# The head of a two-layer decoder trunk: some first loads move from SyncE's queue to ScalarE's, SiLU moves behind a PSUM product, and the order of the first products and splits is written out

## The chip, the core and the metric

The kernel runs on one NeuronCore of one Trainium2 chip, in one launch. Its time is the device time in microseconds (us) of that launch; three runs of the kernel before gave 1242.72, 1240.34 and 1240.87 us, median 1240.87 us. The profile is one execution recorded by the hardware profiler, with its own time and with the span from its first instruction to its last. The engines are TensorE (PE in the profile, with its weight loads apart as PEld), VectorE (DVE), ScalarE (ACT), GpSimd (POOL) and SyncE (SP). SyncE computes nothing; in the kernel before every load of the stage that is looked at here is issued from its queue.

## The reference

The function is a hybrid decoder trunk of two layers on one sequence of 256 tokens with 2048 channels, in float32. The part that matters here is the adaLN step in front of layer 0: three vectors of 2048 are computed from the conditioning vector `c`, and two of them scale and shift `x` ahead of the first big product.

```python
def _adaln(c, w, b):
    mod = jax.nn.silu(c) @ w + b
    shift, scale, gate = jnp.split(mod, 3, axis=-1)
    return shift[:, None, :], scale[:, None, :], gate[:, None, :]

# layer 0
h = x * (1.0 + scale) + shift
proj = h @ in_w                      # (256, 2048) @ (2048, 10304)
z, xBC, dt = jnp.split(proj, ...)
...                                  # convolution, chunked state-space scan, gate, norm
y = y @ out_w
x = _layer_norm(DEEPNORM_ALPHA * x + (1.0 + gate) * y, ln_g[0], ln_b[0])
...                                  # shared K/V, layer 1 (dilated attention), output
```

## The kernel before

Weights are read from memory once, in float32. Each weight piece is 128 partitions by 1024 floats (512 KB). It is loaded into a tile `raw`, and split into two reduced-precision tiles: ScalarE writes the high part `whi` (L100), VectorE the remainder `wlo` (L102). The activations are split in the same way (`hhi` and `hlo`, the two halves of the tile `actT`). A product is then three TensorE passes: high by high, high by low, low by high (L151 to L153 where the channels end on partitions, L213 to L215 where the tokens do).

**Channels.** The 2048 channels of `x` are 16 tiles of 128, numbered `kt`. For every `kt` the function `h_step` runs twice: once for the scale column and once for the shift column of the modulation. A column is a 1 MB tile `araw` of adaLN weights; VectorE multiplies it by `cb_` (SiLU of `c`, spread over all 128 partitions) and adds up along the row (`ada_dot`, L296). For the very first column this is done in two halves of 1024 (L471 and L473), so that the first half needs only half of `cb_`. After the shift column the biases are added (L301), and ScalarE makes `htmp`, that is `x` scaled and shifted (L492), and its high part (L494); VectorE makes the low part (L496).

**Spreading c.** `c` comes as 16 rows of 128 with a 16 by 16 unit matrix beside it (`crow`, the tile called `prm` in the profile). Sixteen small TensorE products with a column of that unit matrix as stationary side (L443) copy each of the 16 rows to all 128 partitions, into four PSUM tiles `cps`; ScalarE copies them into `cb_` (L446). In the kernel before, SiLU is applied to `crow` first (L72), and the products take its result. Around them `warm` issues products of a tile of ones, whose results nobody reads (L435).

**First products.** The function `plain` (L541) multiplies the first channel tile (`kt` = 0) of the first three weight pieces in full float32, straight from `raw` and `htmp`, with no split. Only the second half of those pieces (`kt` = 1) is split, by `half` (L549 and L550). From then on the loop at L623 takes the pieces in the order of the list `order`; between pieces it calls `h_step`, so that channel tiles come into being while products with the earlier ones run. This goes on until about 171 us; then come the scan, the output product, shared K/V, layer 1 and the output.

**What sets the order.** Each engine executes its instructions in the order in which the program gives them to it; a planner may move an instruction of one engine ahead of another of the same engine unless `tc.issue_after(x)` pins it behind `x`. Each queue of loads is served by one engine: a load that must wait for a buffer or for an earlier load holds all loads behind it on the same engine. Each load signals one of eight counters (`DMAHW0` to `DMAHW7` in the listings); the next load that uses the same counter waits for the one before it. Buffers: `raw` has six, `araw` two in each of the pools `wp1` and `pe`, `whi` and `wlo` four each.

The fills at the head are in `fetch` (an `araw`), `fetch_x` (two channel tiles of `x`, 256 KB), `begin_piece` and `end_piece` (the two 256 KB halves of a piece) and `fetch_piece` (a whole piece). The biases are `adab_` (48 KB).

## Time and profile before

| | us |
|---|---|
| median of three runs | 1240.87 |
| lowest and highest run | 1240.34 and 1242.72 |
| time of the profiled execution | 1241.06 |
| its span, first to last instruction | 1239.3 |
| TensorE busy in the span | 1227.7 (99%) |
| VectorE busy | 1026.7 (83%) |
| ScalarE busy | 702.1 (57%) |
| first product with split operands (L151) | starts at 22.03 |

The profiled execution lies 0.19 us above the median of the runs. A timeline row gives start, length, engine, line, operation, output and inputs, how many instructions of the kind it merges, and in brackets the idle time of the engine just before it and what ended it. TensorE's busy time counts the products of ones as well, so 99% doesn't mean that 99% is needed work. A row of stretches gives, for each, the busy time of PE, PEld, DVE, ACT and POOL with the number of instructions, the granted TensorE clock (1.00 is full), the mean busy share of the 16 DMA engines, and what they moved in GB/s. An SPq row is SyncE issuing a load: its length is the time to issue, not the time to land.

### The profile page before, as it was taken

Reading aid. Unit: us, or ns where it says so; the run is one execution under the profiler, and the core shown is the slowest. Engines: PE = TensorE matmul, PEld = TensorE weight load, DVE = VectorE, ACT = ScalarE, POOL = GpSimd, SP = SyncE. Lnnn points to the kernel's source line nnn. Section 1 sums busy time; section 2 is a strip of 40 time slices with the busy share of each in tenths; the row PEclk is TensorE's granted clock in tenths of the full one; section 3 lists DMA queues with packets and bytes.
Section 4 is the critical chain, followed back from the end, with each engine's and each line's share of the span. In section 5 each row is a group of like instructions: output and inputs, shape, how many; then the busy total and the mean of one; then the engine's idle time right before and its main releaser. Section 6 shows DMA issues by size and latency. Waiting matters only on the chain.

```text
span 1239.3 us, 18924 instructions
## 1 busy us (share of the span) xinstructions
PE 1227.7 (99%) x7178; PEld 1056.4 (85%) x7178; DVE 1026.7 (83%) x1454; ACT 702.1 (57%) x1048; POOL 3.8 (0%) x8
## 2 busy tenths in 40 slices
PE   9999999999999999999999999999999999999998
PEld 9889998898888888887888788888888888888886
DVE  6999986999987989899768678889978867658776
ACT  4555477868597789764335544434445645445631
POOL 0000000000000000000000000000000000000001
PEclk9999999999999999999999999999999999999999
DMA  9999977687656456699998569989997784464753
GB/s 368 422 421 422 421 256 248 231 288 257 215 192 210 164 172 202 215 338 338 365 317 294 193 201 354 372 340 369 381 384 293 231 260 136 134 203 121 226 217 68
DMA packets 81051, 335.90 MB, mean 271 GB/s; under 512 B 9168, under 2 KB 9408, under 8 KB 68160
## 3 DMA queue, kind: packets, MB, share of 16 engines
q1 hardware_dynamic: 80384, 333.65, 74.9%
q0 software_dynamic: 576, 1.05, 0.6%
q8 instruction: 56, 0.92, 0.3%
q14 instruction: 35, 0.29, 0.1%
HBM read 331.43 MB, written 3.23 MB: 270 GB/s over the span
## 4 chain that ended last, share of the span: by engine, by line
PE 89%; DMA 4%; DVE 4%; ACT 2%; issue 1%; DVEq 0%; SPq 0%; ACTq 0%
PE acc L182 24%; PE acc L214 12%; PE acc L215 12%; PE acc L213 12%; PE acc L185 12%; PE acc L151 3%; PE acc L153 3%; PE acc L152 3%; DMA raw<-in_win 2%; DMA araw<-in_ada 1%; PE py L758 1%; DVE wlo L102 1%; DVE araw L296 1%; ACT whi L100 1%; PE acc L968 1%
## 5 line engine op out<-in xcount | busy, mean ns | idle before, releaser
L100 ACT ACTIVATE whi<-raw 128x1024 fp32r<-128x1024 f32 x389 | 408.1, 1058 | 359.3 <-PE acc L215 140.7
L102 DVE TENSOR_TENSOR wlo<-raw,whi 128x1024 fp32r<-128x1024 f32 x389 | 469.4, 1223 | 141.5 <-ACT whi L100 137.4
L182 PE MATMUL acc<-actT,whi 128*128 128x512 f32 x1280 | 405.3, 397 | 0.0
L185 PEld LDWEIGHTS acc<-actT,wlo 128*128 128x128 f32 x1280 | 239.4, 188 | 55.6 <-DVE wlo L102 0.4
L214 PE MATMUL acc<-wlo,actT 128*128 128x512 f32 x656 | 257.1, 392 | 1.4 <-DVE wlo L102 1.4
L213 PE MATMUL acc<-whi,actT 128*128 128x512 f32 x656 | 253.6, 394 | 0.0
L185 PE MATMUL acc<-actT,wlo 128*128 128x256 f32 x1280 | 252.8, 279 | 0.0
L296 DVE SCALAR_TENSOR_TENSOR araw<-araw,cb__72 128x2048 f32<-128x2048 f32 x95 | 217.0, 2287 | 3.7 <-DMA araw<-in_ada 3.4
L182 PEld LDWEIGHTS acc<-actT,whi 128*128 128x128 f32 x1280 | 195.9, 189 | 0.4
L215 PE MATMUL acc<-whi,actT 128*128 128x512 f32 x432 | 168.9, 391 | 0.0
L214 PEld LDWEIGHTS acc<-wlo,actT 128*128 128x128 f32 x656 | 123.2, 188 | 27.6 <-DVE wlo L102 2.6
L213 PEld LDWEIGHTS acc<-whi,actT 128*128 128x128 f32 x656 | 122.8, 188 | 24.2
L151 PE MATMUL acc<-actT,whi 128*128 128x256 f32 x372 | 105.0, 285 | 0.9 <-ACT whi L100 0.9
L152 PE MATMUL acc<-actT,whi 128*128 128x256 f32 x372 | 104.4, 283 | 0.0
L153 PE MATMUL acc<-actT,wlo 128*128 128x256 f32 x372 | 102.5, 284 | 1.6 <-DVE wlo L102 1.6
L215 PEld LDWEIGHTS acc<-whi,actT 128*128 128x128 f32 x432 | 81.1, 188 | 16.7
L215 PE MATMUL acc<-whi,ylo 128*128 128x512 f32 x224 | 87.6, 391 | 0.0
L151 PEld LDWEIGHTS acc<-actT,whi 128*128 128x128 f32 x372 | 71.3, 192 | 1.9 <-ACT whi L100 1.3
L153 PEld LDWEIGHTS acc<-actT,wlo 128*128 128x128 f32 x372 | 70.0, 192 | 2.2 <-DVE wlo L102 2.0
L152 PEld LDWEIGHTS acc<-actT,whi 128*128 128x128 f32 x372 | 71.3, 192 | 0.3
L215 PEld LDWEIGHTS acc<-whi,ylo 128*128 128x128 f32 x224 | 42.1, 188 | 8.6
L716 ACT ACTIVATE seg<-cbc,cumT 128x128 f32<-128x128 f32 x128 | 41.0, 389 | 4.9 <-DVE wlo L102 2.3
(289 smaller groups left out, 1159.6 us busy)
## 6 DMA issues: line engine op xcount, KB each, us to landing
araw<-in_ada SPq DMA_DIRECT2D x96, 1024.0 KB, 7.3
raw<-in_win SPq DMA_DIRECT2D x109, 512.0 KB, 6.1
raw<-in_wout SPq DMA_DIRECT2D x64, 512.0 KB, 5.8
raw<-in_wbin SPq DMA_DIRECT2D x64, 512.0 KB, 3.8
raw<-in_wxs SPq DMA_DIRECT2D x48, 512.0 KB, 4.5
raw<-in_wv SPq DMA_DIRECT2D x48, 512.0 KB, 6.2
raw<-in_wk SPq DMA_DIRECT2D x48, 512.0 KB, 7.4
cbc<-cumd SPq DMA_DIRECT2D x16, 512.0 KB, 4.7
```

The costliest lines, as they stand in the source:

```text
L100: copied.append(S.activation(hi, raw, AF.Copy))
L102: latest.append(V.tensor_tensor(lo, raw, hi.bitcast(F32), op=ALU.subtract))
L151: T.matmul(o, hi[:, k, c_], ahi[:, kt, :], start=first, stop=False, skip_group_check=True)
L152: T.matmul(o, hi[:, k, c_], alo[:, kt, :], start=False, stop=False, skip_group_check=True)
L153: T.matmul(o, lo[:, k, c_], ahi[:, kt, :], start=False, stop=kt == k1 - 1, skip_group_check=True)
L182: T.matmul(ps[n], hi[:, k, n * P:n * P + P], both(kt), start=kt == 0, stop=False, skip_group_check=True)
L185: T.matmul(ps[n][:, 0, :], lo[:, k, n * P:n * P + P], high(kt), start=False, stop=kt == KT - 1, skip_group_check=True)
L213: T.matmul(o, h_, hi[:, k, :], start=kt == k0, stop=False, skip_group_check=part)
L214: T.matmul(o, h_, lo[:, k, :], start=False, stop=False, skip_group_check=part)
L215: end = T.matmul(o, l_, hi[:, k, :], start=False, stop=kt == k1 - 1, skip_group_check=part)
L296: return V.scalar_tensor_tensor(raw, raw, 1.0, cb_, op0=ALU.mult, op1=ALU.mult, accum_out=mod[layer][:, ct, j:j + 1])
L716: S.activation(seg[:, hh, b, :], cbc[:, hh, b, :], AF.Relu, bias=cumT[:, b, h0 + hh:h0 + hh + 1], scale=-1.0)
```

## The change

All of it lies in the first 25 us of the program; behind that, the engines get the same instructions in the same order.

- **Queues.** The loads of `c`, of the first two channel tiles of `x`, of the biases and of the first halves of pieces 0 and 1 are issued from ScalarE. SyncE starts with four `araw` one behind the other, then the first half of piece 2, then the second halves.
- **SiLU.** `c` goes into the spreading products as it is; SiLU is applied when ScalarE takes the four PSUM tiles into `cb_`, in place of the copy.
- **Products.** `warm` and `plain` return their last product and take the one that they must come behind, so TensorE's order at the head is the written one: 6 products of ones, 16 spreading products, 13 of ones, the plain products of pieces 0 and 1, 4 of ones, those of piece 2, 4 of ones. In the source the counts were 6, 20, 5 and 5, free to be moved.
- **Splits.** `half` is divided into `high_half` (ScalarE) and `low_half` (VectorE). The high halves of pieces 0 and 1 come ahead of the second channel tile on ScalarE, and their low halves ahead of the low part of that channel tile on VectorE.
- One `fetch_piece` comes ahead of the plain products in the source; its place in SyncE's queue is the same.

```diff
-    nc.sync.dma_start(crow, c)
-    S.activation(crow[:, :P], crow[:, :P], AF.Silu)
+    nc.scalar.dma_start(crow, c)
...
-                def warm(n, at):
+                def warm(n, at, after=None):
                     for _ in range(n):
-                        T.matmul(at[:, 0, :P], ones, ones, start=True, stop=True)
+                        with tc.issue_after(after.ins) if after is not None else ExitStack():
+                            after = T.matmul(at[:, 0, :P], ones, ones, start=True, stop=True)
+                    return after
...
-                warm(6, at)
+                last = warm(6, at)
...
-                            T.matmul(cps[:, j * P:j * P + P],
-                                     crow[:, P + 4 * n + j:P + 4 * n + j + 1].to_broadcast([KT, P]),
-                                     crow[:, :P], start=True, stop=True)
-                        S.activation(cb_[:, 512 * n:512 * n + 512], cps, AF.Copy)
-                    warm(20, at)
+                            with tc.issue_after(last.ins):
+                                last = T.matmul(cps[:, j * P:j * P + P],
+                                                crow[:, P + 4 * n + j:P + 4 * n + j + 1].to_broadcast([KT, P]),
+                                                crow[:, :P], start=True, stop=True)
+                        S.activation(cb_[:, 512 * n:512 * n + 512], cps, AF.Silu)
+                    last = warm(13, at, last)
...
-                    nc.sync.dma_start(xts[kt // 2], xT[:, kt:kt + 2, :])
+                    (nc.sync if kt else nc.scalar).dma_start(xts[kt // 2], xT[:, kt:kt + 2, :])
...
-                    nc.sync.dma_start(pieces[i][:, :512], source[order[i][0]][order[i][1]][:, :512])
+                    (nc.scalar if i < 2 else nc.sync).dma_start(pieces[i][:, :512], source[order[i][0]][order[i][1]][:, :512])
...
-                fetch()
-                fetch()
                 fetch_x(0)
-                nc.sync.dma_start(adab_, par[:, :NB])
+                nc.scalar.dma_start(adab_, par[:, :NB])
                 begin_piece(0)
                 begin_piece(1)
-                fetch()
-                fetch()
+                for _ in range(4):
+                    fetch()
                 begin_piece(2)
...
-                plain(0)
-                plain(1)
+                last = plain(1, plain(0, last))
                 while late:
                     pin[0] = late.pop()().ins
-                fetch_piece()
-                warm(5, first[1][0])
-                plain(2)
-                warm(5, first[1][0])
+                last = warm(4, first[1][0], plain(2, warm(4, first[1][0], last)))
                 h_step()
-                h_step()
-                with tc.issue_after(h_step.bias.ins), tc.issue_after(h_step.high.ins):
-                    half(0)
-                while late:
+                high_half(0)
+                high_half(1)
+                with tc.issue_after(copied[-1].ins):
+                    h_step()
+                with tc.issue_after(h_step.bias.ins):
+                    low_half(0)
+                with tc.issue_after(latest[-1].ins):
+                    low_half(1)
+                with tc.issue_after(latest[-1].ins):
                     pin[0] = late.pop()().ins
-                with tc.issue_after(pin[0]):
-                    half(1)
-                    half(2)
+                with tc.issue_after(h_step.high.ins), tc.issue_after(pin[0]):
+                    high_half(2)
+                    low_half(2)
```

SyncE's queue at the head of the program, before (`prm` is `c`, `xt` the channel tiles of `x`, `adab` the biases, a 128x512 `raw` half a piece; in brackets the counters that a load waits for):

```order
L71 DMA prm<-in_c 16x144
L289 DMA araw<-in_ada 128x2048 x2
L460 DMA xt<-in_xT 128x512
L556 DMA adab<-in_par 128x96
L527 DMA raw<-in_win 128x512 x2
L289 DMA araw<-in_ada 128x2048
L289 DMA araw<-in_ada 128x2048 [waits DMAHW0_49]
L527 DMA raw<-in_win 128x512 [waits DMAHW1_49]
L530 DMA raw<-in_win 128x512 [waits DMAHW2_49]
```

And in the changed kernel:

```order
L288 DMA araw<-in_ada 128x2048 x3
L288 DMA araw<-in_ada 128x2048 [waits DMAHW0_49]
L529 DMA raw<-in_win 128x512 [waits DMAHW1_49]
L532 DMA raw<-in_win 128x512 [waits DMAHW2_49]
L532 DMA raw<-in_win 128x512 [waits DMAHW3_49]
L532 DMA raw<-in_win 128x512 [waits DMAHW4_49]
L93 DMA raw<-in_win 128x1024 [waits DMAHW5_49]
L288 DMA araw<-in_ada 128x2048 [waits DMAHW6_49,DVE_49]
```

Five loads have left SyncE's queue, and its first load is now the first `araw`. The counters 0, 2, 3, 4 and 5 for which it waits are those of the loads that ScalarE issues.

ScalarE's queue at the same place, before:

```order
L72 ACT_TABLE_LOAD
L72 ACTIVATE prm<-prm 16x128 [waits DMAHW0_49]
L446 ACTIVATE cb__72<-cps 128x512 [waits PE_49] x4
L492 ACTIVATE htmp<-xt,mod_84 128x256 [waits DMAHW3_49,DVE_49]
L494 ACTIVATE actT<-htmp 128x256 [waits Activation_49]
L492 ACTIVATE htmp<-xt,mod_84 128x256 [waits DVE_49]
L494 ACTIVATE actT<-htmp 128x256 [waits Activation_49]
L549 ACTIVATE whi<-raw 128x512 [waits DMAHW2_49]
```

And in the changed kernel:

```order
L71 DMA prm<-in_c 16x144
L462 DMA xt<-in_xT 128x512
L560 DMA adab<-in_par 128x96
L529 DMA raw<-in_win 128x512 x2
L448 ACT_TABLE_LOAD
L448 ACTIVATE cb__72<-cps 128x512 [waits PE_49] x4
L494 ACTIVATE htmp<-xt,mod_83 128x256 [waits DMAHW2_49,DVE_49]
L496 ACTIVATE actT<-htmp 128x256 [waits Activation_49]
L551 ACTIVATE whi<-raw 128x512 [waits DMAHW2_49]
L551 ACTIVATE whi<-raw 128x512 [waits DMAHW3_49]
L494 ACTIVATE htmp<-xt,mod_83 128x256 [waits DVE_49]
L496 ACTIVATE actT<-htmp 128x256 [waits Activation_49]
```

Five loads stand in front, the small SiLU is gone, and two high halves, which wait for the second halves of pieces 0 and 1 (SyncE's loads at L532), stand ahead of the second channel tile.

TensorE's queue, before (products of `ones` are the ones whose results nobody reads):

```order
L435 MATMUL acc<-ones 128x128 x10
L443 MATMUL cps<-prm 128x128 x16
L435 MATMUL acc<-ones 128x128 x23
L541 MATMUL acc<-htmp,raw 128x256 x8
L435 MATMUL acc<-ones 128x128 x3
L541 MATMUL acc<-htmp,raw 128x256 x4
L151 MATMUL acc<-actT,whi 128x256
L152 MATMUL acc<-actT,whi 128x256
```

And in the changed kernel:

```order
L435 MATMUL acc<-ones 128x128 x6
L445 MATMUL cps<-prm 128x128 x16
L435 MATMUL acc<-ones 128x128 x13
L544 MATMUL acc<-htmp,raw 128x256 x8
L435 MATMUL acc<-ones 128x128 x4
L544 MATMUL acc<-htmp,raw 128x256 x4
L435 MATMUL acc<-ones 128x128 x4
L150 MATMUL acc<-actT,whi 128x256
L151 MATMUL acc<-actT,whi 128x256
```

Ahead of the spreading products stand 6 products of ones instead of 10, behind them 13 instead of 23, and 4 and 4 instead of 3 and none around the plain products of piece 2. The profile shows each product of the head as two records.

More of the change, by code (lines that the diff above doesn't have):

```diff
@@ L532, in trunk, with plain @@
                 begin, done, ended, halves = {}, set(), [], {}
-                def plain(i):
+                def plain(i, after):
                     k = order[i][0]
@@ L540, in plain, with high_half, low_half @@
                     for n in range(4):
-                        T.matmul(pss[k][n // 2][:, n % 2, :], pieces[i][:, n * P:n * P + P], plain.t,
-                                 start=n % 2 == 0, stop=False, skip_group_check=True)
-                def half(i):
+                        with tc.issue_after(after.ins):
+                            after = T.matmul(pss[k][n // 2][:, n % 2, :], pieces[i][:, n * P:n * P + P], plain.t,
+                                             start=n % 2 == 0, stop=False, skip_group_check=True)
+                    return after
+                def high_half(i):
                     halves[i] = [wp.tile([P, 1024], F32R, name=n, bufs=4) for n in ("whi", "wlo")]
-                    hi, lo = (t[:, 512:1024] for t in halves[i])
-                    raw = pieces[i][:, 512:1024]
-                    copied.append(S.activation(hi, raw, AF.Copy))
-                    latest.append(V.tensor_tensor(lo, raw, hi.bitcast(F32), op=ALU.subtract))
+                    copied.append(S.activation(halves[i][0][:, 512:], pieces[i][:, 512:], AF.Copy))
+                def low_half(i):
+                    hi, lo = (t[:, 512:] for t in halves[i])
+                    latest.append(V.tensor_tensor(lo, pieces[i][:, 512:], hi.bitcast(F32), op=ALU.subtract))
                     halves[i] = [t.rearrange("p (k n) -> p k n", k=2) for t in halves[i]]
-                fetch()
-                fetch()
                 fetch_x(0)
-                nc.sync.dma_start(adab_, par[:, :NB])
+                nc.scalar.dma_start(adab_, par[:, :NB])
                 begin_piece(0)
                 begin_piece(1)
-                fetch()
-                fetch()
+                for _ in range(4):
+                    fetch()
                 begin_piece(2)
@@ L569, in trunk @@
                 fetch()
+                fetch_piece()
                 plain.t = h_step.t
[L571 to L572 removed]
+                last = plain(1, plain(0, last))
                 while late:
                     pin[0] = late.pop()().ins
[L575 to L578 removed]
+                last = warm(4, first[1][0], plain(2, warm(4, first[1][0], last)))
                 h_step()
[L580 to L583 removed]
+                high_half(0)
[7 more added lines that the diff above has]
+                with tc.issue_after(latest[-1].ins):
                     pin[0] = late.pop()().ins
[L585 to L587 removed]
+                with tc.issue_after(h_step.high.ins), tc.issue_after(pin[0]):
+                    high_half(2)
+                    low_half(2)
                 fetch_piece()
```

## The prediction

> **What bounds the kernel now.** I read the page first, then the stretches of the head, the chain that ended last, the waits, and the timelines of the first 25 us engine by engine.
>
> ```profile
> span 1239.3 us, 18924 instructions
> PE 1227.7 (99%) x7178; PEld 1056.4 (85%) x7178; DVE 1026.7 (83%) x1454; ACT 702.1 (57%) x1048; POOL 3.8 (0%) x8
> ```
>
> TensorE has 11.6 us without work in the whole span. A change at the head can give only what the head wastes, so the stretches come next.
>
> ```profile
> 0.00:2.00 2.00, 0.94 (x4) 0.95 (x5) 0.17 (x2) 1.27 (x1) 0.20 (x4) 1.00 0.02 5
> 2.00:4.00 2.00, 2.00 (x12) 2.00 (x11) 0.00 (x0) 0.33 (x2) 0.00 (x0) 1.00 0.85 238
> 7.00:12.00 5.00, 5.00 (x35) 4.78 (x34) 2.86 (x5) 2.35 (x4) 0.00 (x0) 0.74 0.99 334
> 12.00:58.00 46.00, 44.13 (x299) 40.77 (x298) 41.62 (x49) 24.21 (x37) 0.00 (x0) 0.99 1.02 421
> ...
> 22.03:58.68 36.65, 34.10 (x234) 31.35 (x233) 34.66 (x38) 22.24 (x34) 0.00 (x0) 1.00 1.02 421
> 58.68:182.00 123.32, 123.32 (x823) 113.98 (x824) 113.33 (x129) 70.72 (x91) 0.00 (x0) 1.00 0.97 387
> ```
>
> From 58.68 to 182 us TensorE is never idle: whatever moves its work at 58.68 us moves the end by as much. Between its first split product (22.03 us) and 58.68 us it is idle for 36.65 - 34.10 = 2.55 us, while the DMA engines are full (share 1.02, 421 GB/s). The chain says who ends that stage:
>
> ```profile
> 0.74 0.40 SPq L71
> 1.20 5.01 DMA araw<-in_ada
> 6.23 12.92 DMA raw<-in_win
> 34.00 13.02 DMA araw<-in_ada
> 47.04 2.31 DVE araw L296 x2
> 57.40 1.24 DVE wlo L102
> 58.68 0.39 PE acc L153
> ```
>
> The chain runs through landings: a column lands at 47.02 us, 13 us after it was issued, because everything issued before it is still going through full DMA engines. Behind it VectorE works nearly without a gap until the split that releases TensorE at 58.68 us. The waits from 20 to 58.8 us agree:
>
> ```profile
> ACT whi L100 <- DMA raw<-in_win: 12.9, 5, 4.2
> DVE wlo L102 <- ACT whi L100: 1.6, 3, 0.6
> ```
>
> So the time at 58.68 us is set by how early the DMA stream gets through its bytes; VectorE is close behind (34.66 of 36.65 us busy); TensorE has slack.
>
> **The change part by part: the DMA stream.** The bytes are the same, so it can only start sooner or run fuller in the first 12 us.
>
> - Start: the first `araw` is issued at 1.20 us, behind `c` at 0.74. With `c` on ScalarE it is issued at 0.74: 0.46 us gained.
> - Ramp: from 2 to 4 us the engines move 238 of 421 GB/s, a loss of 2 x (1 - 238/421) = 0.87 us.
> - Small rows: from 7 to 12 us they move 334, a loss of 5 x (1 - 334/421) = 1.03 us. This is when `x`, the biases and the half pieces come through.
>
> Two queues may fill these holes in part. The most is 0.46 + 0.87 + 1.03 = 2.36 us. The other end is a loss: no row shows two queues of loads side by side, and if their turns cost once more what the small rows cost, it is 1.03 - 0.46 = 0.57 us late. Between them I am guided by the DMA share: 0.85 and 0.99 while so little was moved. The engines were occupied, by rows that the change keeps. So I count a good third of 1.90 us, 0.7, as filled: 0.46 + 0.7 = 1.2 us gained (estimate).
>
> **TensorE, the spreading and SiLU.**
>
> ```profile
> 1.05 4.63 PE L435 MATMUL acc<-ones 128*128 128x128 f32 x20 [1.05 <-DVE magic L248]
> 5.62 4.08 PE L443 MATMUL cps<-prm 16*128 16x128 f32 x32
> 9.63 6.89 PE L435 MATMUL acc<-ones 128*128 128x128 f32 x46
> 16.36 3.62 PE L541 MATMUL acc<-htmp,raw 128*128 128x256 f32 x16
> 19.82 0.83 PE L435 MATMUL acc<-ones 128*128 128x128 f32 x6
> 20.49 1.89 PE L541 MATMUL acc<-htmp,raw 128*128 128x256 f32 x8
> 22.03 0.47 PE L151 MATMUL acc<-actT,whi 128*128 128x256 f32 x1
> ...
> 9.20:9.40 0.20, 0.20 (x4) 0.95 0.82 246
> 12.60:12.80 0.20, 0.20 (x3) 0.52 1.36 574
> ```
>
> The first 20 records take (5.62 - 1.05)/20 = 0.229 us each; the spreading ones 4.08/32 = 0.128. TensorE thus starts slow, although the clock column says 1.00 there, and the clock falls to half between 9.2 and 12.8 us. Six products of ones are 12 records: they end at 1.05 + 12 x 0.229 = 3.79 us, and spreading starts 1.83 us sooner. At the pace of before it ends at 7.87; at the slow pace it takes 32 x 0.229 = 7.33 us and ends at 11.12, 1.42 later than the 9.70 of before. I take the early value, since most of spreading ran fast in this trace, and keep both.
>
> ```profile
> 0.73 1.28 ACT L72 ACT_TABLE_LOAD   x1 [0.73 <-PEq L1306]
> 6.96 0.60 ACT L446 ACTIVATE cb__72<-cps 128x512 f32<-128x512 f32 x1 [4.36 <-PE cps L443]
> 14.23 0.60 ACT L492 ACTIVATE htmp<-xt,mod 128x256 f32<-128x256 f32 x1 [3.89 <-DVE mod L301]
> 20.39 0.60 ACT L492 ACTIVATE htmp<-xt,mod 128x256 f32<-128x256 f32 x1 [5.11 <-DVE mod L301]
> 21.35 1.66 ACT L549 ACTIVATE whi<-raw 128x512 fp32r<-128x512 f32 x3
> ...
> 10.37 1.23 DVE L473 SCALAR_TENSOR_TENSOR araw<-araw,cb__72 128x1024 f32<-128x1024 f32 x1 [0.65 <-ACT cb__72 L446]
> 21.48 0.42 DVE L496 TENSOR_TENSOR actT<-htmp,actT 128x256 fp32r<-128x256 f32 x1 [1.11 <-ACT actT L494]
> 21.99 1.90 DVE L550 TENSOR_TENSOR wlo<-raw,whi 128x512 fp32r<-128x512 f32 x3
> ...
> 2.12 0.43 SPq L460 DMA_DIRECT2D xt<-in_xT  x1
> 2.59 0.67 SPq L556 DMA_DIRECT2D adab<-in_par  x1
> 3.30 1.05 SPq L527 DMA_DIRECT2D raw<-in_win  x2
> ...
> L415 ACT ACTIVATE sz<-acc x4: 591/597/597, 334.0 to 515.0; 128x512 f32<-128x512 f32 x4
> ```
>
> - SiLU for copy: SiLU out of PSUM at 128x512 is 597 ns (L415), the copy 0.60: nothing. The small SiLU stood beside products of ones: nothing.
> - Five issues on ScalarE: 0.40 + 0.43 + 0.67 + 1.05 = 2.55 us at SyncE's prices, then the table load: 0.73 + 2.55 + 1.28 = 4.56 us. The first `cps` is there at 3.79 + (6.96 - 5.62) = 5.13 at the earliest: hidden, with 0.57 us to spare, beyond which it delays VectorE's first columns.
> - VectorE: its column halves wait for `cb_`, so they move by -1.83 to +1.42 us. Ahead of L496 it was idle for 1.11 us; two low halves (2 x 0.63 = 1.27) now fill that. By the third piece it stands at -2.94 to +0.31. Since it gets no piece before it lands, only the plus end reaches the total: between 0 and +0.3 in place of the gain.
> - Plain products: they started at 16.36, behind ones, though `htmp` was ready at 14.83. They can now start at about 13.0, or 16.3 at the slow pace. Behind that stand 3.62 + 1.89 and 16 records of ones at some 0.14 (0.83/6), 2.2 us: 7.7 in all, so the first split product comes at 20.7 to 24.0 instead of 22.03. Even +2.0 lies inside the 2.55 us of slack: nothing on the path.
> - High halves ahead of `htmp` on ScalarE: they wait for the second half of piece 1. The half ahead of it landed at 19.15 (6.23 + 12.92), so two more of 262 KB at 421 GB/s give 20.4 us, and 1.2 less in the changed kernel: 19.2, plus 0.55 (1.66/3) is 19.75, against `htmp` at 20.39. Behind it are queued `htmp` and its high part, for which L496 and the first split products wait. If the stream gained only 0.46 it would be 20.5, 0.1 late, inside TensorE's slack: nothing.
> - SyncE: waits for counters of ScalarE's loads. Its second half of piece 0 waits for `x`. With four `araw` ahead (4.2 MB, 10 us of DMA) this starves nothing unless `x` takes longer than those: nothing.
>
> Sum: -1.2 us. The profiled execution is 1241.06 us, its span 1239.3 with 1.76 around it, so 1239.9 on its scale; it is 0.19 above the median, so against 1240.87 the forecast is 1239.7 us.
>
> **The rivals.**
>
> *Two queues move no more than one.* The share of 0.99 at 334 GB/s speaks for it, the 0.85 of the ramp against. Only the 0.46 us of issue remains: 1240.4 us. [...]
>
> *The holes fill altogether.* 421 GB/s from 2 us on is 2.36 us, and with VectorE up to 2.9 us ahead some of its 1.6 us of waits for ScalarE goes too, say 0.4: 2.8 us, 1238.1. For it: VectorE's lead; against it: the shares again.
>
> *The slow clock stays through the spreading: slower.* The place is TensorE's 16 spreading products. For it: they feed 16 rows only, and the half clock came right after 3.4 us of mostly them; now 2.74 us of ones stand ahead in place of 4.57, which may not lift the clock at all. Then `cb_` is whole 1.42 us late and VectorE, +0.31 after filling its gap, sets the stage: 1241.2 us. From the point where the first split product comes after 22.03 + 2.55 = 24.6 us TensorE adds to it: each 3.4 us of half clock that reaches the plain products costs 1.7, so 24.0 + 1.7 = 25.7 gives 1.1 more, 1242.3; two such stretches 1244. Against it: ones and plain products are full arrays, and the clock rose over ones at 12.8.
> [...]
>
> **How the numbers follow.** Forecast (-0.5 to -2.0) 0.40; no more than one queue 0.18; holes filled 0.17; slow clock 0.23, of which 0.07 beyond its point; something I have not seen, slower, 0.02. What a measurement of this kernel can tell from no change is about 0.2%, 2.5 us: 1238.4 to 1243.4. Only the filled holes pass it downwards (0.17) and the far part of the slow clock and the unseen upwards (0.09); 0.74 lies within. The range 1238.0 to 1242.0 leaves out about half of the filled holes and the far part of the slow clock. The forecast's own range is 1238.9 to 1240.4.
>
> **What would show it.** Right: the first `araw` issued near 0.74; more than 334 GB/s from 7 to 12 us; `htmp` near 12.5 to 13.5; TensorE unbroken from about 57.5 instead of 58.68. Wrong: GB/s of the first 12 us as before (one queue's worth); spreading records at 0.229 us and `cb_` after 10.4 (slow clock); ScalarE waiting for the second halves beyond 20.5; the first split product after 24.6.

## The result: a little slower, and the profile after

The changed kernel takes 1243.51 us (median of 20 runs, 1241.69 to 1245.29) against 1241.01 for the kernel before (20 runs beside them, 1240.13 to 1243.84). The ratio is 1.0018 with a 95% interval of 1.0011 to 1.0025, which is 2.2 us (1.4 to 3.1). The forecast was 1239.7 us, with a range up to 1242.0. The profiled execution of the changed kernel took 1243.62 us.

The head of its page, and then its stretches (columns as in the prediction: the busy times of TensorE, of its weight loads, of VectorE, ScalarE and GpSimd, then the granted clock, the DMA share and GB/s):

```profile
span 1241.8 us, 18886 instructions
PE 1229.2 (99%) x7160; PEld 1057.8 (85%) x7160; DVE 1026.7 (83%) x1454; ACT 702.8 (57%) x1047; POOL 3.8 (0%) x8
```
```profile
2.00:4.00 2.00, 2.00 (x11) 1.76 (x9) 0.00 (x0) 0.58 (x1) 0.00 (x0) 1.00 0.81 304
4.00:7.00 3.00, 3.00 (x14) 3.00 (x15) 0.00 (x0) 1.30 (x2) 0.00 (x0) 1.00 0.99 399
7.00:12.00 5.00, 5.00 (x24) 4.78 (x23) 1.45 (x3) 1.79 (x3) 0.00 (x0) 1.00 1.00 380
12.00:17.00 5.00, 5.00 (x25) 4.99 (x24) 3.85 (x8) 1.02 (x2) 0.00 (x0) 1.00 1.01 402
17.00:18.00 1.00, 1.00 (x6) 0.89 (x5) 1.00 (x2) 0.42 (x1) 0.00 (x0) 1.00 0.68 258
18.00:19.00 1.00, 1.00 (x7) 0.87 (x6) 1.00 (x1) 0.85 (x2) 0.00 (x0) 1.00 0.97 158
19.00:20.00 1.00, 1.00 (x6) 0.90 (x5) 1.00 (x3) 0.00 (x0) 0.00 (x0) 1.00 0.90 328
```

The first 12 us went as hoped: 304 GB/s instead of 238 from 2 to 4 us and 380 instead of 334 from 7 to 12. Added up packet by packet, the changed kernel had moved 0.36 MB more than before by 14 us. Then something new shows: from 17 to 20 us the engines move 258, 158 and 328 GB/s. By 26 us the changed kernel is 0.31 MB behind, by 42 us 0.53 MB. The kernel before has no such hole: it moved 421 GB/s from 12 to 58 us.

What SyncE waited for in the first 30 us of the changed kernel, and its queue there:

```profile
SPq L532 <- DMA xt<-in_xT: 3.7, 1, 3.7
SPq L532 <- DMA raw<-in_win: 2.8, 1, 2.8
...
SPq L532 <- DMA adab<-in_par: 2.4, 1, 2.4
...
SPq L93 <- DMA raw<-in_win: 1.8, 2, 1.0
```
```profile
0.74 3.49 SPq L288 DMA_DIRECT2D araw<-in_ada  x4
5.70 0.33 SPq L529 DMA_DIRECT2D raw<-in_win  x1
9.78 6.22 SPq L532 DMA_DIRECT2D raw<-in_win  x3
17.05 0.33 SPq L93 DMA_DIRECT2D raw<-in_win  x1
17.50 0.36 SPq L288 DMA_DIRECT2D araw<-in_ada  x1
```

The first column is issued at 0.74 us, as forecast. But the three second halves (L532) wait for `x`, the biases and a half piece, all loads of ScalarE's queue: they go out between 9.78 and 16.00 us, only 0.26 MB each. The fourth piece waits once more, for the second half piece of ScalarE's queue, and goes out at 17.05; the fifth column follows at 17.50. In the meantime SyncE's earlier loads had been used up: that is the hole. Why those loads were so late is in the table of DMA issues of the first 20 us (KB each, median us from issue to landing) and in the queues' packets from 8 to 14 us:

```profile
raw<-in_win ACTq DMA_DIRECT2D x2, 256.0 KB, 13.8
xt<-in_xT ACTq DMA_DIRECT2D x1, 256.0 KB, 8.6
adab<-in_par ACTq DMA_DIRECT2D x1, 48.0 KB, 10.9
```
```profile
q1 hardware_dynamic: 286, 2.06, 83.0%
q10 hardware_dynamic: 288, 0.31, 16.5%
```

Both queues sent equally many packets, 286 and 288; but one of SyncE's holds 2.06 MB / 286 = 7.2 KB on average and one of ScalarE's 0.31 MB / 288 = 1.1 KB. ScalarE's loads therefore got 0.31 of 2.37 MB, and its last half piece landed at about 17 us.

The other rows that answer to the prediction's: TensorE's head, the copies into `cb_`, VectorE's wait for a column, and the release of TensorE, which was 58.68 us before.

```profile
1.05 2.93 PE L435 MATMUL acc<-ones 128*128 128x128 f32 x12 [1.05 <-DVE magic L247]
3.93 7.19 PE L445 MATMUL cps<-prm 16*128 16x128 f32 x32
11.05 5.91 PE L435 MATMUL acc<-ones 128*128 128x128 f32 x26
...
23.68 0.36 PE L150 MATMUL acc<-actT,whi 128*128 128x256 f32 x1
...
60.19 0.38 PE L152 MATMUL acc<-actT,wlo 128*128 128x256 f32 x1 [1.14 <-DVE wlo L101]
```
```profile
3.42 1.28 ACT L448 ACT_TABLE_LOAD   x1 [3.42 <-issue]
...
11.16 0.60 ACT L448 ACTIVATE cb__72<-cps 128x512 f32<-128x512 f32 x1 [1.11 <-PE cps L445]
...
17.58 1.27 ACT L551 ACTIVATE whi<-raw 128x512 fp32r<-128x512 f32 x2 [0.89 <-DMA raw<-in_win]
21.81 0.60 ACT L494 ACTIVATE htmp<-xt,mod 128x256 f32<-128x256 f32 x1 [2.96 <-DVE mod L300]
```
```profile
24.36 1.23 DVE L101 TENSOR_TENSOR wlo<-raw,whi 128x1024 fp32r<-128x1024 f32 x1 [0.26 <-ACT whi L99]
...
35.33 2.29 DVE L295 SCALAR_TENSOR_TENSOR araw<-araw,cb__72 128x2048 f32<-128x2048 f32 x1 [0.65 <-DMA araw<-in_ada]
```

The release comes 1.51 us later. Two suspects stand in these rows. The spreading ran at 7.19/32 = 0.225 us per record, the slow pace of the prediction's third rival, and `cb_` was whole 1.4 us late. And SyncE stood still, after which VectorE waits for columns (0.65 us at 35.33; before, it waited for none from 5 to 58 us).

### The profile page after: what moved, and what is told of

It reads as the page before. It is cut to its first block, busy times and chain, and to the rows that moved or that the text cites. A ratio compares the mean times of both kernels' runs of the same rounds, so it can differ in the third digit from the quotient of the medians.

```text
span 1241.8 us, 18886 instructions
## 1 busy us (share of the span) xinstructions
PE 1229.2 (99%) x7160; PEld 1057.8 (85%) x7160; DVE 1026.7 (83%) x1454; ACT 702.8 (57%) x1047; POOL 3.8 (0%) x8
## 4 chain that ended last, share of the span: by engine, by line
PE 88%; DVE 5%; DMA 4%; ACT 2%; issue 1%; SPq 0%; DVEq 0%; ACTq 0%
PE acc L181 24%; PE acc L213 12%; PE acc L214 12%; PE acc L184 12%; PE acc L212 12%; PE acc L150 3%; PE acc L152 3%; PE acc L151 3%; DMA araw<-in_ada 2%; PE py L764 1%; DVE araw L295 1%; DVE wlo L101 1%; ACT whi L99 1%; DMA raw<-in_wv 1%; PE acc L974 1%
```

## The experiments

Two measures stand beside the time. The *release* is the start of the product of the last row of TensorE above. The *lag* is how far VectorE is behind the kernel before: the median difference in start between the same instructions (same operation and tiles, counted in order), those that start from 60 to 70 us. Ratios are of the time, to the kernel before on the same chip, with 95% intervals.

| kernel | release, us | lag, us | ratio |
|---|---|---|---|
| changed | 60.19 | +1.30 | 1.0018 (1.0011 to 1.0025) |
| changed, again | 60.54 | +1.76 | 1.0018 (1.0009 to 1.0027) |
| ten ones | 60.59 | +1.70 | 1.0015 (1.0006 to 1.0024) |
| loads back | 58.27 | -0.61 | 1.0000 (0.9992 to 1.0009) |
| loads back, ten ones | 57.99 | -0.66 | 0.9999 (0.9990 to 1.0008) |
| half pieces back, ten ones | 58.12 | -0.66 | 0.9997 (0.9989 to 1.0006) |
| other counters | 57.73 | -1.09 | 0.9995 (0.9986 to 1.0004) |
| c and SiLU alone | 60.23 | +1.34 | 1.0007 (0.9998 to 1.0016) |
| order alone | 58.33 | -0.56 | 1.0000 (0.9991 to 1.0009) |
| hold alone | 58.22 | -0.67 | 1.0003 (0.9994 to 1.0012) |
| hold, longer | 61.20 | +2.31 | 1.0022 (1.0013 to 1.0031) |
| other counters, ten ones | 57.22 | -1.48 | 1.0001 (0.9992 to 1.0009) |
| the same, again | 57.82 | -0.94 | 0.9994 (0.9985 to 1.0003) |
| c and SiLU, ten ones | 58.96 | +0.07 | 1.0005 (0.9997 to 1.0014) |
| before, again | 59.04 | +0.15 | 0.9999 (0.9990 to 1.0008) |

### Is it the clock or the queue?

Four kernels. The first changes the pace alone:

```diff
-                last = warm(6, at)
+                last = warm(10, at)
```

> The changed kernel, with ten products of ones ahead of the spreading in place of six; its queues stay as they are. Two theories. CLOCK: the spreading ran at 0.225 us per record because too few full products stand ahead of it; cb_ was whole 1.4 us late, VectorE with it, and so the release of TensorE (58.68 before, 60.19 after). Then ten products (20 records, 4.6 us) give back the pace of before: spreading from 5.6 to 9.7 us, the last copy into cb_ at about 9.7 instead of 11.16, release at 58.7 or sooner, time within 0.6 us of before. QUEUE: SyncE was held at the second halves (issued at 9.78, 12.56 and 15.67 us) by counters of the loads on ScalarE's queue; the DMA engines then ran short at 17 to 20 us and every later landing is 1.2 to 1.5 us late. Then the spreading gets its pace back all the same, but SyncE's second halves and the hole at 17 to 20 us stay where they are, the release is at 60.0 to 60.3, and the time stays 1.3 to 2.5 us above before.

The second takes x, the biases and the half pieces back to SyncE, in the places that they had before, and leaves six products of ones:

```diff
-                    (nc.sync if kt else nc.scalar).dma_start(xts[kt // 2], xT[:, kt:kt + 2, :])
+                    nc.sync.dma_start(xts[kt // 2], xT[:, kt:kt + 2, :])
...
-                    (nc.scalar if i < 2 else nc.sync).dma_start(pieces[i][:, :512], ...)
+                    nc.sync.dma_start(pieces[i][:, :512], ...)
...
+                fetch()
+                fetch()
                 fetch_x(0)
-                nc.scalar.dma_start(adab_, par[:, :NB])
+                nc.sync.dma_start(adab_, par[:, :NB])
                 begin_piece(0)
                 begin_piece(1)
-                for _ in range(4):
-                    fetch()
+                fetch()
+                fetch()
```

> The changed kernel with only c left on ScalarE's queue: x, the biases and the two half pieces are back on SyncE, in the places that they had before. Six products of ones. QUEUE: no second half waits for a counter, no hole at 17 to 20 us (over 400 GB/s in each us), the stream is 0.46 us ahead of before, release between 58.2 and 58.9, time between 0.6 us below before and 0.3 above, though the spreading is still slow (0.225 us per record, last cb_ at about 11.2). CLOCK: with the slow spreading VectorE is still 1.4 us late and the release stays at about 60.2, time 1.3 to 2.5 us above before.

The third is the second with `warm(10, at)`; the fourth has ten ones too, with c, x and the biases on ScalarE's queue and only the half pieces back on SyncE:

```diff
-                last = warm(6, at)
+                last = warm(10, at)
...
-                    (nc.scalar if i < 2 else nc.sync).dma_start(pieces[i][:, :512], ...)
+                    nc.sync.dma_start(pieces[i][:, :512], ...)
...
                 fetch_x(0)
                 nc.scalar.dma_start(adab_, par[:, :NB])
+                fetch()
+                fetch()
                 begin_piece(0)
                 begin_piece(1)
-                for _ in range(4):
-                    fetch()
+                fetch()
+                fetch()
```

> Only c on ScalarE's queue and ten products of ones: both suspected causes are gone, so both theories expect the release at 58.7 us or sooner (by the 0.46 us of earlier issue, 58.2) and a time between before and 0.6 us below it. If it is as slow as the changed kernel, neither theory holds, and the order of the first products or of the halves is at fault.

> c, x and the biases on ScalarE's queue, the half pieces on SyncE, ten products of ones. QUEUE: x (1 KB rows, taking turns with 8 KB rows of the columns) lands at 9 to 10 us and the biases at 10 to 12, so SyncE is held at the second halves until then, some 4 us shorter than in the changed kernel; the hole is smaller or gone, release 58.2 to 59.2, time 0.5 us below to 0.6 above before. CLOCK: the same as with only c on ScalarE's queue, since the pace is restored: at or up to 1.2 us below before.

With ten ones and the changed queues, the spreading ran from 5.59 to 9.8 us and SyncE stood as in the changed kernel: the loss stayed whole (release 60.59, a little beyond the 60.3 expected at most). TensorE's spreading and one of the us of the hole in that kernel:

```profile
5.59 4.20 PE L445 MATMUL cps<-prm 16*128 16x128 f32 x32
```
```profile
18.00:19.00 1.00, 1.00 (x6) 0.87 (x5) 1.00 (x3) 0.99 (x2) 0.00 (x0) 1.00 1.07 172
```

With the loads back, the spreading was as slow as in the changed kernel, the hole was gone, and so was the loss:

```profile
3.93 7.19 PE L445 MATMUL cps<-prm 16*128 16x128 f32 x32
```
```profile
18.00:19.00 1.00, 1.00 (x6) 0.89 (x5) 1.00 (x1) 0.91 (x2) 0.00 (x0) 1.00 1.09 440
```

So it is the queues, not the pace. With x and the biases alone on ScalarE's queue, SyncE still waited 3.4 us for `x`, but with four columns and three half pieces issued ahead of it, and with 1.2 us of waiting (for the biases) behind it, and nothing was lost (release 58.12, 436 GB/s from 18 to 19 us): here the loads ahead of the wait outlasted it.

### Standing still, or the second queue itself?

The waits come from the counters on which the loads report. In the traces of before and of the changed kernel they are eight (71 transfers land on the first and 70 on each of the others; four more counters take one each at the end). At the head they are dealt out in turn in the order in which the program ranks the loads of both queues, and a load waits until the one eight before it has landed: in the changed kernel `x` landed at 9.76 us, the biases at 12.55, the half pieces at 15.66 and 17.04, and the second halves and the fourth piece were issued at 9.78, 12.56, 15.67 and 17.05. So what SyncE waits for can be changed without moving any load: here three columns are ranked ahead of x, the biases and the half pieces.

```diff
-                    (nc.sync if kt else nc.scalar).dma_start(xts[kt // 2], xT[:, kt:kt + 2, :])
+                    x = (nc.sync if kt else nc.scalar).dma_start(xts[kt // 2], xT[:, kt:kt + 2, :])
+                    if not kt:
+                        first_x.append(x)
+                        tc.add_manual_dep(x.ins, loads[2].ins.name, mybir.DependencyInfo(
+                            mybir.DependencyClass.NoSync, mybir.DependencyReason.DATA), reason="counters")
...
+                for _ in range(4):
+                    fetch()
                 fetch_x(0)
-                nc.scalar.dma_start(adab_, par[:, :NB])
-                begin_piece(0)
-                begin_piece(1)
-                for _ in range(4):
-                    fetch()
+                with tc.issue_after(first_x[0].ins):
+                    nc.scalar.dma_start(adab_, par[:, :NB])
+                    begin_piece(0)
+                    begin_piece(1)
```

> The changed kernel with every load on the queue and in the turn that it has there; only the counters are dealt out otherwise: three columns get theirs ahead of x, the biases and the two half pieces, so that the first two second halves wait for columns and only the third for x. (One column product stands ahead of two splits on VectorE instead of behind them; the rest of the order is the same.) Two theories of the hole at 17 to 20 us. HOLD: it comes from SyncE standing still for the counters of late loads. Then the second halves are issued by 10.5 us, every us from 17 to 20 moves over 380 GB/s, the bytes moved by 22 us are 0.1 to 0.4 MB ahead of before (0.3 MB behind in the changed kernel), TensorE is released at 57.6 to 58.6 us, and the time is 1.2 us below before to 0.4 above. TURNS: it comes from the second queue itself, whose rows take turns with the columns' rows. Then the hole stays under whatever counters, the release is at 59.5 or later, and the time is 1.0 to 2.5 us above before.

SyncE's queue and the hole's three us in this kernel:

```profile
9.90 3.58 SPq L543 DMA_DIRECT2D raw<-in_win  x3
13.52 0.43 SPq L93 DMA_DIRECT2D raw<-in_win  x1
16.03 0.33 SPq L290 DMA_DIRECT2D araw<-in_ada  x1
```
```profile
17.00:18.00 1.00, 1.00 (x7) 0.87 (x6) 1.00 (x2) 0.25 (x1) 0.00 (x0) 1.00 1.09 426
18.00:19.00 1.00, 1.00 (x6) 0.88 (x5) 1.00 (x1) 0.99 (x2) 0.00 (x0) 1.00 1.05 428
19.00:20.00 1.00, 1.00 (x6) 0.89 (x5) 1.00 (x3) 0.02 (x1) 0.00 (x0) 1.00 1.04 438
```

The second halves did not all go out by 10.5 us, as expected, but by 13.5; that was early enough. Same loads on the same queues, no hole, 0.28 MB ahead of before, release 57.73. The second queue as such cost nothing here. One more thing differs in this kernel: VectorE takes the next column product at 23.62 us, ahead of two splits (in the changed kernel it comes behind them, at 25.50) and the one after it ahead of a third, and ScalarE takes a split ahead of some copies out of PSUM.

```profile
23.62 2.29 DVE L297 SCALAR_TENSOR_TENSOR araw<-araw,cb__72 128x2048 f32<-128x2048 f32 x1 [0.25 <-DMA araw<-in_ada]
```

That order may have a share of its own: behind these instructions the next bias is added at 30.92 us, and at 31.52 with the loads back, where the splits come first. So up to 0.6 us of the release may be this order's.

The opposite test puts the standing still into a kernel that has no second queue of loads: the second kernel above (loads back), with the three second halves made to wait for VectorE's first two column products and first bias. The lines left out name these gates and put the first two steps ahead of the loads in the source; VectorE's order of work stays that of the kernel with the loads back.

```diff
-                    nc.sync.dma_start(pieces[i][:, 512:], source[order[i][0]][order[i][1]][:, 512:])
+                    hold(nc.sync.dma_start(pieces[i][:, 512:], source[order[i][0]][order[i][1]][:, 512:]), gates[i])
...
+                def hold(load, gate):
+                    tc.add_manual_dep(load.ins, gate.ins.name, mybir.DependencyInfo(
+                        mybir.DependencyClass.Sync, mybir.DependencyReason.DATA), reason="hold")
```

> Only c on ScalarE's queue (the kernel with x, biases and half pieces back on SyncE), and the three second halves made to wait, on SyncE, for VectorE's first two column products and its first bias: issued at about 9.6, 13.0 and 15.6 us, as in the changed kernel (9.78, 12.56, 15.67), with no second queue of loads. HOLD: the hole comes back without the second queue (some us between 15 and 20 under 350 GB/s), the release goes to 59.3 to 60.3 and the time to 0.8 to 2.5 us above before. TURNS: without the second queue the engines stay full, release at 58.0 to 58.6, time within 0.6 us of before.

```profile
9.62 6.33 SPq L537 DMA_DIRECT2D raw<-in_win  x3
15.99 0.42 SPq L93 DMA_DIRECT2D raw<-in_win  x1
```

Neither expectation came true whole. The engines were short, 324 GB/s from 17 to 18 us and 381 to 19, as HOLD said, but the release stayed at 58.22, as TURNS said. This hold ended 1.06 us sooner than that of the changed kernel: the fourth piece went out at 15.99 instead of 17.05. So the next kernel holds that piece too, for VectorE's first low part.

```diff
                 fetch_piece()
+                tc.add_manual_dep(loads[-1].ins, gates[3].name, mybir.DependencyInfo(
+                    mybir.DependencyClass.Sync, mybir.DependencyReason.DATA), reason="hold")
```

> The kernel with the hold alone, in which the piece behind the three second halves is held too, for VectorE's first low part (about 17.2 us; it was issued at 15.99 there, and at 17.05 in the changed kernel). With the shorter hold the engines were short by some 0.2 MB and the release did not move (58.22). HOLD: another 1.1 to 1.2 us of standing still takes 0.3 to 0.5 MB more, so that columns come later than VectorE asks for them (rows of waits of araw for its landing), release 58.8 to 59.8, time 0.3 to 1.8 us above before. If the release stays at 58.1 to 58.4, standing still is not enough, and the second queue has a part of its own in the loss.

SyncE, VectorE's wait for columns from 5 to 59 us, and the release:

```profile
9.62 6.33 SPq L539 DMA_DIRECT2D raw<-in_win  x3
17.16 0.33 SPq L95 DMA_DIRECT2D raw<-in_win  x1
```
```profile
DVE araw L297 <- DMA araw<-in_ada: 1.4, 3, 0.6
```
```profile
61.20 0.38 PE L154 MATMUL acc<-actT,wlo 128*128 128x256 f32 x1 [0.89 <-DVE wlo L103]
```

With 1.17 us more of standing still the loss is there, larger than expected (61.20, not 58.8 to 59.8), and the time is that of the changed kernel: 1.0022 to 1.0018. Bytes fell from 0.04 MB ahead of before (at 26 us, shorter hold) to 0.56 behind. With the loads back the loss goes, and it goes too with the second queue kept and the counters changed (there with that other order of a few instructions). Put in alone, and for long enough, it comes. Standing still is the cause, and it has a point from which it costs: in these kernels between 15.99 and 17.16 us for the fourth piece.

### What the other parts are worth

c on ScalarE's queue and SiLU out of PSUM, on the kernel before with its order and its other loads:

```diff
-    nc.sync.dma_start(crow, c)
-    S.activation(crow[:, :P], crow[:, :P], AF.Silu)
+    nc.scalar.dma_start(crow, c)
...
-                        S.activation(cb_[:, 512 * n:512 * n + 512], cps, AF.Copy)
+                        S.activation(cb_[:, 512 * n:512 * n + 512], cps, AF.Silu)
```

> The kernel before with c alone on ScalarE's queue and SiLU taken as the spread c leaves PSUM; its order of fills, first products and halves stays. START: the first column is issued at 0.74 in place of 1.20 us and all landings move by 0.46: release of TensorE at 58.0 to 58.4, time 0.3 to 0.7 us below before, which the runs can hardly tell from nothing. If the 0.66 us that the kernel with c alone and ten ones was ahead after 60 us came from the new order instead, the release stays at 58.6 to 58.8.

And the new order alone, which is the kernel with the loads back and in it c on SyncE and its SiLU ahead of the spreading, as before:

```diff
-    nc.scalar.dma_start(crow, c)
+    nc.sync.dma_start(crow, c)
+    S.activation(crow[:, :P], crow[:, :P], AF.Silu)
...
-                        S.activation(cb_[:, 512 * n:512 * n + 512], cps, AF.Silu)
+                        S.activation(cb_[:, 512 * n:512 * n + 512], cps, AF.Copy)
```

> The changed kernel's order of fills, spread, first products and halves with the loads of before: c too on SyncE, its SiLU before the spreading. START: nothing gained, nothing lost: release at 58.5 to 58.9, time within 0.6 us of before, though spreading comes right behind six products of ones and is slow. If the new order is what helps, the release is at 58.2 or sooner; if it costs, 59.0 or later.

Both surprised. The first was released at 60.23, 1.55 us late, though it moved 0.2 MB more than before by 14 us. The second was ahead by 0.35 us at the release (lag -0.56), though its stream stood within 0.06 MB of before at every point. In both the spreading follows six ones and takes 7.19 us. The first again with `warm(10, at)`:

> The kernel with c on ScalarE's queue and SiLU out of PSUM alone, with ten products of ones ahead of the spreading in place of six. CLOCK: its loss (VectorE 1.4 us late from 20 us on, released at about 60.2) came from the slow spreading alone, since in the order of before nothing takes up that delay. Then the last copy into cb_ is back at 9.7 us or sooner, and the release at 58.0 to 58.8: the lower end if the earlier issue of the first column (0.46 us) counts, the upper if it counts for nothing. Time 0.7 us below before to 0.3 above. If the release stays at 59.8 or later, it is not the pace but SiLU out of PSUM or c's other queue.

Its last copy into `cb_` is at 9.81 us and its release at 58.96: the slow pace was the whole loss. In the order of before it costs 60.23 - 58.96 = 1.27 us; in the new order next to nothing (loads back, six ones against ten: 58.27 and 57.99, lag -0.61 and -0.66). There two low halves stand where VectorE used to wait for ScalarE: its waits for `actT` from 5 to 58 us fall from 2.2 to 1.1 us, and a late start is partly taken up. The release of 58.96 lies a little above what was expected (58.8 at most), between the two profiles of before (58.68 and 59.04): the earlier stream gave nothing there.

The mean granted clock of every run adds something on the kernel before. Of the sixteen profiles, the six with 0.999 or above all have the slow spreading, and the eight with the fast one are all below. Of the 33 runs of before beside c and SiLU alone, five are at 0.999 (1242.31 to 1243.03 us) and 28 below (median 1240.42), so some executions of before probably have the slow spreading too, though no profile caught one. With the new order alone eight of eleven runs are at 0.999 or above, and took 1239.95 to 1241.72 us: there the slow pace hardly shows in the time.

### Once more, and the fastest head

The changed kernel as it is, and the kernel with other counters and in it `warm(10, at)`:

> The changed kernel once more, as it is. The loss at the head should be there in every execution: release at 59.9 to 60.5, VectorE 1.1 to 1.6 us behind before from 60 to 195 us. The further 1.1 us that the first profile lost between the store of cumd and the loads of cbc (4.73 us from issue to issue against 3.22 in before; 3.4 to 4.6 in the other kernels) should not repeat by rule: anything between 3.2 and 4.8, in which nothing of the change has a part. Time 1.2 to 2.6 us above before.

> The changed kernel with the counters dealt out otherwise and ten products of ones ahead of the spreading. No hole, and VectorE starts its columns 1.4 us sooner than with six. If the stream is what sets the release now, little comes of the pace: release 57.3 to 57.8 (57.73 with six), time 0.4 to 1.6 us below before. If VectorE's late start was still what set it there, 56.9 to 57.3. If the release is later than 57.9, the fast pace costs something that I have not seen.

The changed kernel repeats, a little later than expected (60.5 at most): release 60.54, ratio 1.0018. Other counters with ten ones have the earliest release of all, 57.22, below the range of the first case and within the second; VectorE now waits 1.2 us for a column, so both stream and pace are used up. But its time did not follow (1.0001). Therefore the kernel before, as it is, and this one were taken once more:

> The kernel before, unchanged, for a second profile of it. If the first profile was released later than usual, this one has the release at 57.7 to 58.4 (58.68 in the first), and the other kernels' times then stand to their releases as they should. If the release is again at 58.6 to 58.8, the head does not vary, and some 0.7 us of what a kernel gains at the head is lost on the way to the end. The store of cumd and the loads of cbc may lie anywhere from 2.7 to 4.8 us apart. Time 0.5 us to either side of before.

> The kernel with other counters and ten ones once more. Its head gained 1.5 us (release 57.22) and its time nothing (+0.4 us by the medians, interval 1.0 below to 1.1 above before). If that was scatter, the release is again at 57.0 to 57.5 and the time 0.3 to 1.5 us below before. If the gain is given back, the release is the same, VectorE's lead of 1.4 us shrinks to under 0.7 somewhere between 60 us and the end, in a place other than the round trip of cumd, and the time is within 0.6 us of before.

The second profile of before was released at 59.04, so the first was not a late one. The fastest head came at 57.82 this time, and its time at 0.9994 (0.9985 to 1.0003). That it is faster than before is not shown: its eleven runs all have a mean granted clock below 0.999 (median 1240.67 us), and the 14 of 21 runs of before beside them that are below 0.999 have a median of 1240.45. It is faster than the changed kernel: 1241.09 us, with an interval that ends at 1.0009, beside 1243.43 on the same chip, with one that begins there, and no run of the one reaches the other (1241.64 at most, 1242.37 at least). Where its lead goes can be seen in one place, the round trip of `cumd` through memory, here in before and in that kernel:

```profile
198.22 0.51 SPq L695 DMA_DIRECT2D cumd<-araw  x1
201.44 0.81 SPq L711 DMA_DIRECT2D cbc<-cumd  x2
```
```profile
197.19 0.50 SPq L714 DMA_DIRECT2D cumd<-araw  x1
201.42 0.82 SPq L730 DMA_DIRECT2D cbc<-cumd  x2
```

The store goes out 1.03 us sooner and the loads 0.02. VectorE's lag in this kernel is -1.02 us just ahead of that (196 to 204 us) and -0.22 behind it (207 to 230). So the expectation that the lead is not lost there was wrong. From issue to issue the trip took 2.70 to 4.73 us over the sixteen profiles, with no sign of what sets it: 3.22 and 3.71 in before, 4.73 and 3.80 in the changed kernel, 4.29 and 4.23 in this one. Whether a lead at the head is lost there by rule stays open.

## Why the prediction was wrong

- **SyncE's waits, "nothing": the step that failed.** It was argued that four columns ahead, 10 us of DMA, cover the wait unless `x` takes longer. `x` did not (9.78 us). But behind it the next two second halves waited in their turn for the biases and for a half piece, and the fourth piece for the other half piece, which landed after 10.9 and 13.8 us (the half pieces' median), and the first three waits let out only 0.26 MB each. The cover had to be reckoned against the last of the waits, at 17.05 us, and not the first: by then 6.09 MB had been issued (four columns, seven loads of 256 KB, `c` and the biases) and all but 0.3 MB of it moved. In the shorter hold, which cost nothing, 0.8 MB were left when the fourth piece went out at 15.99. In place of nothing the waits cost 1.92 us at the release against the loads back (58.27 to 60.19, the same order on VectorE) and 2.46 against the other counters (57.73), of which up to 0.6 may be that kernel's order.
- **The DMA stream, -1.2.** Its first 14 us were right in sign: 0.36 MB, 0.86 us at 421 GB/s, of which the earlier start gave about 0.18 MB (what the kernel with the loads back had moved more), 0.43 us of the 0.46 forecast. The ramp and the small rows gave the other half, 0.4 instead of 0.7; that the holes fill altogether (2.36 us) did not come.
- **"The time at 58.68 us is set by how early the DMA stream gets through": only half true.** With c and SiLU alone and ten ones the stream was 0.2 MB ahead throughout and the release no earlier. With the new order alone it was the other way round. VectorE, which the prediction had "close behind", was the limit as much.
- **The clock, early value taken: wrong.** The slow pace came in all eight profiles with six ones; the spreading ended at 11.05 (11.12 in the rival). That rival had the slow spreading and its +0.31 for VectorE (24.36 against 23.99 us, +0.37), but not the cause of the time; the half clock that it put into the plain products did not come (the clock is 1.00 from 0 to 30 us of the changed kernel).
- **Nothing on the path: right.** ScalarE's table load began at 3.42 us and held up no copy by more than TensorE did; the first split product came at 23.68, inside 20.7 to 24.0; the high halves ended at 18.85, ahead of `htmp` at 21.81.
- **The rival that two queues move no more than one: nearly right on bytes, silent on the loss.** Beyond the earlier start the two queues were 0.18 MB ahead at 14 us, 0.4 us of stream; with the other counters 0.28 against 0.19 MB (loads back) at 22 us, 0.2 us. That loads on the second queue come late was not in the rival.

The time: the prediction's 1239.7 had -1.2 for the head. Measured against it at the release are +1.51 and +1.86 in two profiles, so 2.7 to 3.1 us of the 3.8 by which the forecast missed the median are the head's, and 1.9 to 2.5 us of that the one step. The rest, about 1 us, lies within the spread of single executions and the round trip of `cumd`; in the second profile of the changed kernel VectorE's lag also grew from 1.76 us to 3.19 (196 to 204 us), and its split products of 128x256, 0.28 us a record at 60.88 us, took 0.42 from 61.39 us on, just behind the release. Whether the one made the other is not shown.

## What to carry to other kernels

Before a load goes to a second queue, ask who will wait for its counter, and follow the whole row of loads behind that: here SyncE stood, wait behind wait, until the last of the late loads had landed at 17.04 us, and what covered it were the 6.09 MB issued ahead of the last wait. Small rows on a queue beside one with large rows landed late here, while the two sent equally many packets and not equally many bytes (286 and 288 packets, 2.06 and 0.31 MB). A gain in bytes early on was worth nothing here once a later wait let the engines run dry (0.36 MB ahead at 14 us, 158 GB/s from 18 to 19, 0.31 MB behind at 26), so read GB/s over the whole stretch and not only where the change was made.

## What was not expected of the hardware

- Two queues of loads sent equally many packets, 286 and 288 from 8 to 14 us, though they held 7.2 and 1.1 KB on average. 256 KB of `x` took 8.6 us to land on the second queue, where only `c` stood ahead of it; on SyncE's queue in the kernel before, behind two columns, it took 8.0.
- In eight profiles 7.19 us of products that feed 16 rows left TensorE at its slow pace. Behind 12 records of full products the spreading took 0.225 us per record to its end (eight profiles), behind 20 it took 0.128 to 0.155 on average (4.08 to 4.95 us for 32, eight profiles), and the clock column reads 1.00 for the slow case. The full products behind the slow spreading began slow as well: 26 records in 5.91 us in the changed kernel, 0.227 each. What decides the pace of an execution is not shown.
- The same store and load of `cumd` took 2.70 to 4.73 us from issue to issue in kernels that do not differ there.
